# Convolution taps four to a product, with twofold tiles made by DMA, layer norm read from PSUM, and joint first attention scores

## The chip, the cores and the metric

The kernel runs on one core of one Trainium2 chip. The metric is the device time of one execution in microseconds (us). The engines are TensorE (PE, with weight loads shown apart as PEld), VectorE (DVE), ScalarE (ACT), GpSimd (POOL) and SyncE (SP), which only issues DMAs here. Each engine works through its own list of instructions in order and waits for the others by semaphores.

## The reference, cut to what matters

```python
def conformer_conv(h, w_pw1, b_pw1, w_dw, b_dw, ln_g, ln_b, w_pw2, b_pw2):
    u = h @ w_pw1 + b_pw1                     # 512 tokens, 1024 -> 2048
    a, gate = jnp.split(u, 2, axis=-1)
    u = a * jax.nn.sigmoid(gate)
    u = causal_dwconv(u, w_dw, b_dw)          # 31 taps, each feature by itself
    u = jax.nn.silu(layernorm(u, ln_g, ln_b))
    return u @ w_pw2 + b_pw2

for i in range(2):                            # DEPTH = 2
    h = rmsnorm(x, mix_norm_g[i])
    x = x + (conformer_conv(h) if i == 0 else nsa_attention(h))
    x = x + conv_ffn(rmsnorm(x, ffn_norm_g[i]))
```

All is float32 in and out: 512 tokens, 1024 features, 16 heads of 64 in 4 groups. Attention has three branches (compressed, selected, window). With 512 tokens the selected and the window branch each see all earlier tokens, so for each head and each block of 128 queries there are two products of queries with keys, one per branch.

## The kernel before

Activations lie transposed: a tile holds 128 features in its partitions and 512 tokens along its rows, so 1024 features are KT = 8 tiles. A float32 operand of TensorE is split in a high and a low part (ScalarE casts the high part, VectorE subtracts), and `mm3` issues three products: high by high, high by low, low by high.

Four stages follow each other: `conv`, `ffn0`, `attn`, `ffn1`. In `conv`, loop step c projects tile c twice (`project_half`: gate, then value, 24 products each), forms the gated `u` of unit c, and works on the taps of the units before it. The 31 taps of a unit are shared out by the table `CONV`:

- TensorE takes `pe` taps, each as a product with a diagonal matrix, into a `pb` buffer of PSUM (`products`: three products per tap). ScalarE and GpSimd build the diagonals from the identity (`diagonals`, L390 and L393).
- GpSimd takes `pool` taps (`pool_taps`: ScalarE multiplies, L366, GpSimd adds, L368 and L374).
- VectorE takes the rest (`tap`, L345), partly into a `pa` buffer and partly, `late`, on top of TensorE's result.
- `merge` (L405, L406) adds the three sums. It also subtracts the mean of the first unit (`cb`), squares, and GpSimd adds the tiles and squares of units 0 to 6 (L422, L423) for the statistics.

Then comes the layer norm: products with a matrix of 1/1024 and with a column of ones (L490, L493), small vector operations (L502 to L507), a power on GpSimd (L509), a transposition that spreads the result over the partitions, copies of mean and scale from PSUM to SBUF (L499, L511), subtraction, multiplication, Silu, split. The second projection holds all eight outputs in the eight PSUM buffers. `warm` issues products without use in the wait.

PSUM has eight buffers with tags: `pa` 2, `pb` 2, `pf` 3, `po` 1. SBUF slots of 512 columns come from one pool of `NSP` = 55. Within an engine the order of the instructions is set when the kernel is built, by a list scheduler that works with planned durations; the chip keeps this order whatever the durations are. The order of the attention's pieces comes from the table `PLAN`.

In `attn`, `Head.scores` issues for each block of queries the products with the keys of both branches: `G.T` and `G.U` hold two forms of the keys, each branch in its own slot, so that the first two steps have four products each (L1075, L1076). The step's masks and minima follow on VectorE (L1079).

## Time and profile before

| | |
|---|---|
| median of 3 runs | 1302.63 us (1301.27 to 1305.75) |
| the profiled execution | 1305.12 us |
| its span in the trace | 1303.0 us |
| PE busy | 1252.3 us, 96% of the span |
| DVE, ACT, POOL busy | 1034.1, 739.2, 408.2 us |
| `conv` stage | about 0 to 236 us |
| `ffn0`, `attn`, `ffn1` | about 236 to 600, 600 to 937, 937 to 1303 us |

The stages overlap by some us at their borders. Busy time of PE overstates what it does, since matmuls are pipelined: the distance between the starts of two products tells more. A product of 512 columns is shown with 0.39 us, while the next one starts 0.23 us later.

### The profile page before, as it was taken

How to read it: one execution, taken by the hardware profiler on the slowest of the kernel's cores; microseconds unless marked ns; L12 is line 12 of the kernel's file. 1: busy time of each engine (PE TensorE's matmuls, PEld its weight loads, DVE VectorE, ACT ScalarE, POOL GpSimd, SP SyncE). 2: the span in 40 equal slices, each digit the busy share in tenths (PEclk: the TensorE clock that was granted, in tenths of full speed). 3: DMA queues.
4: the chain of work that ended last, by engine and by line, in shares of the span. 5: the costliest groups of instructions: out<-in, count | busy, mean ns of one | idle time of the engine just before them, and what ended most of it. 6: DMA issues, size and time to landing. Idle time of an engine off the chain costs nothing.

```text
span 1303.0 us, 20243 instructions
## 1 busy us (share of the span) xinstructions
PE 1252.3 (96%) x7538; PEld 1105.6 (85%) x7538; DVE 1034.1 (79%) x1777; ACT 739.2 (57%) x1419; POOL 408.2 (31%) x464
## 2 busy tenths in 40 slices
PE   8999789999999999999899999999899999999998
PEld 6887678888999999978888898887688899999996
DVE  6999964689978687775878888888768997778873
ACT  7667733445555455543667778676644465455541
POOL 2668940200200000024557667743220110000000
PEclk9999879999999999999899999999999999999999
DMA  6122102322333232335240101111122232323221
GB/s 232 51 65 65 49 1 81 112 73 81 112 96 112 86 101 97 99 126 156 92 159 35 34 33 34 50 33 41 43 72 79 92 102 92 115 85 126 82 90 73
DMA packets 36946, 109.34 MB, mean 84 GB/s; under 512 B 4208, under 2 KB 4848, under 8 KB 36848
## 3 DMA queue, kind: packets, MB, share of 16 engines
q1 hardware_dynamic: 36848, 108.06, 25.3%
q8 instruction: 59, 0.97, 0.3%
q14 instruction: 39, 0.32, 0.1%
HBM read 103.85 MB, written 2.10 MB: 81 GB/s over the span
## 4 chain that ended last, share of the span: by engine, by line
PE 76%; DVE 11%; POOL 5%; ACT 4%; issue 3%; DMA 1%; SPq 0%; POOLq 0%; ACTq 0%; DVEq 0%
PE pa L631 15%; PE pf L631 7%; PE pb L235 7%; PE pb L236 7%; PE pb L237 6%; PE pf L235 6%; PE pf L236 6%; PE pf L237 6%; PE po L631 4%; POOL s L368 2%; PE pa L237 2%; PE pa L236 2%; PE pa L235 2%; DVE s L231 2%; PE po L1114 2%
## 5 line engine op out<-in xcount | busy, mean ns | idle before, releaser
L646 POOL TENSOR_TENSOR S<-raw 128x512 f32<-128x512 f32 x34 | 53.1, 1562 | 514.3 <-DMA raw<-in_up_dram 297.3
L565 ACT CAST wh<-raw 128x1024 fp32r<-128x1024 f32 (+2 forms) x112 | 95.9, 862 | 84.6 <-PE pb L236 25.5
L566 DVE TENSOR_TENSOR wl<-raw,wh 128x1024 fp32r<-128x1024 f32 (+2 forms) x112 | 114.6, 1030 | 25.8 <-ACT wh L565 25.7
L631 PE MATMUL pa<-s,wh 128*128 128x256 f32 x704 | 129.6, 281 | 0.9 <-ACT wh L565 0.9
L235 PE MATMUL pf<-s,wh 128*128 128x512 f32 x296 | 117.4, 405 | 7.5 <-ACT s L230 3.2
L236 PE MATMUL pf<-s,wh 128*128 128x512 f32 x296 | 118.8, 402 | 0.0
L237 PE MATMUL pf<-s,wl 128*128 128x512 f32 x296 | 118.1, 399 | 0.5 <-DVE wl L225 0.5
L631 PEld LDWEIGHTS pa<-s,wh 128*128 128x128 f32 x704 | 109.9, 189 | 3.5 <-ACT wh L565 1.7
L1090 POOL TENSOR_SCALAR s<-s,cf,gates 128x128 f32<-128x128 f32 (+3 forms) x128 | 79.8, 631 | 79.2 <-DVE cf L1087 66.2
L235 PE MATMUL pb<-s,wh 128*128 128x512 f32 x254 | 99.5, 396 | 2.6 <-ACT s L230 2.4
L236 PE MATMUL pb<-s,wh 128*128 128x512 f32 x254 | 100.3, 395 | 0.0
L237 PE MATMUL pb<-s,wl 128*128 128x512 f32 x254 | 99.8, 394 | 0.0
L631 PE MATMUL pa<-s,wl 128*128 128x256 f32 x352 | 99.1, 281 | 0.0
L224 ACT CAST wh<-raw 128x1024 fp32r<-128x1024 f32 (+1 forms) x60 | 63.2, 1054 | 48.4 <-PE pf L236 28.5
L230 ACT CAST s<-s 128x512 fp32r<-128x512 f32 x84 | 51.7, 619 | 67.2 <-DVE s L580 37.8
L235 PE MATMUL pf<-wh,s 128*128 128x256 f32 (+1 forms) x288 | 83.8, 292 | 4.3 <-DVE v L916 2.6
L1084 ACT ACTIVATE s<-pa,mn 128x128 f32<-128x128 f32 (+3 forms) x128 | 67.4, 531 | 30.1 <-DVE mn L1079 24.0
L236 PE MATMUL pf<-wl,s 128*128 128x256 f32 (+1 forms) x288 | 82.9, 288 | 0.0
L237 PE MATMUL pf<-wh,s 128*128 128x256 f32 (+1 forms) x288 | 82.5, 287 | 0.0
L231 DVE TENSOR_TENSOR s<-s,s 128x512 fp32r<-128x512 f32 x84 | 66.1, 791 | 18.3 <-ACT s L230 18.0
L225 DVE TENSOR_TENSOR wl<-raw,wh 128x1024 fp32r<-128x1024 f32 (+1 forms) x43 | 60.0, 1395 | 22.5 <-ACT wh L224 22.2
L235 PEld LDWEIGHTS pf<-s,wh 128*128 128x128 f32 x296 | 56.4, 191 | 20.8 <-ACT s L230 3.4
(284 smaller groups left out, 3934.1 us busy)
## 6 DMA issues: line engine op xcount, KB each, us to landing
raw<-in_up_dram SPq DMA_DIRECT2D x88, 512.0 KB, 3.6
raw<-in_pw_dram SPq DMA_DIRECT2D x24, 512.0 KB, 3.6
raw<-in_dn_dram SPq DMA_DIRECT2D x48, 256.0 KB, 2.6
raw<-in_dn_dram SPq DMA_DIRECT2D x32, 320.0 KB, 2.8
raw<-in_win_k_dram SPq DMA_DIRECT2D x8, 536.0 KB, 3.5
raw<-in_win_q_dram SPq DMA_DIRECT2D x8, 512.0 KB, 3.5
raw<-in_cw_dram SPq DMA_DIRECT2D x8, 512.0 KB, 3.2
raw<-in_wout_dram SPq DMA_DIRECT2D x8, 512.0 KB, 3.3
```

What stands on the lines that cost most here:

```text
L224: nc.scalar.copy(h[:, :n], raw[:, :n])
L225: (eng or nc.vector).tensor_sub(l[:, :n], raw[:, :n], h[:, :n].bitcast(F32))
L231: nc.vector.tensor_sub(l, src, h.bitcast(F32))
L235: nc.tensor.matmul(out, ah, bh, start=start, stop=False)
L236: nc.tensor.matmul(out, ah, bl, start=False, stop=False)
L237: nc.tensor.matmul(out, al, bh, start=False, stop=stop)
L565: nc.scalar.copy(h, raw)
L566: (eng or nc.vector).tensor_sub(l, raw, h.bitcast(F32))
L631: nc.tensor.matmul(o, p, q, start=start and i + j == 0, stop=i == KT // 2 - 1 and j == 2, skip_group_check=True)
L646: eng[0].tensor_add(s1, a21, a22)
L1084: nc.scalar.activation(a, sv, AF.Exp, scale=-1.0, bias=s.mn[:, c:c + 1], accum_out=s.sums[:, c:c + 1])
L1090: nc.gpsimd.tensor_scalar(a, a, s.cf[:, c:c + 1], gates[:, i, 3 * s.h + 1 + br:3 * s.h + 2 + br], op0=ALU.mult, op1=ALU.mult)
```

## The change

It has four parts.

1. Convolution on TensorE. A product now takes four taps of 64 features. For each unit, `unit` has SP make four twofold tiles (`twice`: two halves of the features, high and low part): the lower 64 partitions hold 64 features, the upper 64 the same features shifted by one token. Each takes two DMAs from SBUF to SBUF and a memset of one column on GpSimd. The weights of such a product have two blocks of output columns, so that it gives two sums, of taps that lie two tokens apart; they land in different partitions, and ScalarE copies them out of two `pa` buffers (L425, L426), one of them to the other half of the partitions, shifted by two tokens. VectorE adds them (`gather`). The weights come from DRAM as `diag` and are split like other weights (L404 to L406), in place of diagonals built on ScalarE and GpSimd. The table changes: TensorE's four-tap groups are 3, 2, 4, 4, 4, 4, 6, 5 per unit (two halves each, three products each), GpSimd's taps 8, 8, 7, 6, 6, 6, 3, 3; VectorE gets the rest.
2. Layer norm from PSUM. Mean and scale are read by VectorE where TensorE left them (`dp`, `rp`), without copies. The last two units go into the statistics by products of their own, instead of an addition on GpSimd. Six outputs of the second projection are held at once, and two follow; a unit is centred into one of two `ctr` buffers, scaled, and split, in turn.
3. Slots. `NSP` falls to 47; `y`, the kept parts of the FFN's combined input (`kept`) and double tiles of the attention (`wide`) have buffers of their own.
4. Attention. The keys of both branches lie side by side in a `wide` tile, and one product covers both branches in the first two steps of a head. The additions in `compress_blocks` take two groups at once.

The core of the diff:

```diff
-CONV = {"pe": [7, 10, 8, 9, 6, 8, 11, 14], "pool": [6, 6, 6, 8, 8, 6, 7, 6], "late": [6, 6, 3, 8, 10, 7, 9, 1], ... "w1": 13, "w2": 9, ...
+CONV = {"pe": [3, 2, 4, 4, 4, 4, 6, 5], "pool": [8, 8, 7, 6, 6, 6, 3, 3], ... "w1": 10, "w2": 6, ...
                 def unit(s, o):
                     c, u = s.c, slot()
                     s.u = u
-                    nc.vector.tensor_mul(u, o, nrm.b)
-                    nc.vector.scalar_tensor_tensor(u, u, v("b_pw1", c), s.y, op0=ALU.add, op1=ALU.mult)
-                    s.uh, s.ul = split(u)
-                    s.sum = ps("pa")
...
+                    nc.vector.tensor_mul(o, o, nrm.b)
+                    nc.vector.scalar_tensor_tensor(u, o, v("b_pw1", c), s.y, op0=ALU.add, op1=ALU.mult)
+
+                    parts = split(u)
+                    s.twice = [[slot(F32R) for _ in parts] for _ in range(2)]
+                    for n, ts in enumerate(s.twice):
+                        for p, t in zip(parts, ts):
+                            rows = p[n * HD:(n + 1) * HD].bitcast(F32)
+                            nc.gpsimd.memset(t[HD:P, 0:1].bitcast(F32), 0.0)
+                            nc.sync.dma_start(t[0:HD, :].bitcast(F32), rows)
+                            nc.sync.dma_start(t[HD:P, 1:S].bitcast(F32), rows[:, 0:S - 1])
...
                 def products(s):
-                    s.pd = ps("pb")
-                    for n, k in enumerate(s.pe):
-                        mm3(s.pd[:, k:S], s.diag[n][0], s.diag[n][1], s.uh[:, 0:S - k], s.ul[:, 0:S - k],
-                            n == 0, n == len(s.pe) - 1)
+
+                    s.pd = [ps("pa") for _ in range(2)]
+                    s.w, s.own = slot(), s.apart and slot()
+                    if not s.apart:
+                        s.sum = ps("pb")
+                    for n in range(2):
+                        for j in range(s.npe):
+                            k = QUAD * j
+                            mm3(s.pd[n][:, k:S], *s.diag[2 * j + n], *(t[:, 0:S - k] for t in s.twice[n]),
+                                j == 0, j == s.npe - 1)
+                        rows = slice(n * HD, (n + 1) * HD)
+                        other = slice((1 - n) * HD, (2 - n) * HD)
+                        if s.apart:
+                            nc.scalar.copy(s.own[rows], s.pd[n][rows])
+                        else:
+                            nc.scalar.activation(s.sum[rows], s.pd[n][rows], AF.Identity, bias=v("b_dw", s.c)[rows])
+                        nc.scalar.copy(s.w[rows, 2:S], s.pd[n][other, 0:S - 2])
+
+                def gather(s):
+                    nc.vector.tensor_add(s.sum[:, 2:S], s.sum[:, 2:S], s.w[:, 2:S])
+                    if s.apart:
+                        nc.vector.tensor_add(s.sum, s.sum, s.own)
...
-                y = units[c].y
-                (nc.vector if c < CONV["sub"] else nc.gpsimd).tensor_sub(y, y, db)
-                nc.vector.tensor_mul(y, y, rb)
...
+            def centre(c):
+
+                cs.append(stage["own"].tile([P, S], F32, tag="ctr", name=nm("ctr"), bufs=NCTR))
+                nc.vector.tensor_sub(cs[c], units[c].y, dp)
+
+            def scale(c):
+                y = cs[c]
+                nc.vector.tensor_mul(y, y, rp)
                 nc.scalar.activation(y, y, AF.Silu, bias=v("ln_b", c), scale=v("ln_g", c))
                 hs.append(split(y))
...
-                        nc.tensor.matmul(sv, q, G.T[br][:, 0:n], start=True, stop=False)
-                        nc.tensor.matmul(sv, q, G.U[br][:, 0:n], start=False, stop=True)
...
+                    for m, t in enumerate((G.T, G.U)):
+                        t = t.rearrange("p (b n) -> p b n", b=2)[:, br:br + nb, 0:n]
+                        nc.tensor.matmul(o[:, 0:nb * n].rearrange("p (b n) -> p b n", b=nb), q, t,
+                                         start=m == 0, stop=m == 1)
```

Where the scheduler puts the work is shown at three places. A name is a tile with its number; two rows with one name touch the same tile.

First TensorE, at the end of the last projection. Before, `pf_1434` is the value half of unit 7, `pb_1398` holds the tap products of unit 6.

```order
L237 MATMUL pf_1434<-s_188,wl_1274 128x512
L235 MATMUL pf_1434<-s_198,wh_1273 128x512
L236 MATMUL pf_1434<-s_199,wh_1273 128x512
L237 MATMUL pf_1434<-s_198,wl_1274 128x512
L236 MATMUL pb_1398<-s_1286,s_1153 128x512
L237 MATMUL pb_1398<-s_1285,s_1154 128x512
```

After, `pf_1357` is the value half of unit 7, `pa_1309` and `pa_1310` hold the sums of unit 6, and `s_1232` and `s_1233` are twofold tiles of unit 6, high and low.

```order
L241 MATMUL pa_1309<-s_1232,dh_1113 128x512
L243 MATMUL pf_1357<-s_188,wl_1222 128x512
L241 MATMUL pf_1357<-s_198,wh_1221 128x512
L242 MATMUL pf_1357<-s_199,wh_1221 128x512
L243 MATMUL pf_1357<-s_198,wl_1222 128x512
L242 MATMUL pa_1309<-s_1233,dh_1113 128x512
```

One product of unit 6 stands ahead of the end of the projection in both, and the rest of unit 6 and all of unit 7 behind it: 74 products before, 65 after.

Second, VectorE behind this point, before: `s_1459` is unit 7's `u`, and `s_1463` its low part.

```order
L355 TENSOR_TENSOR s_1459<-pf_1434,s_270 128x512
L345 SCALAR_TENSOR_TENSOR pa_1289<-s_1282,vec,pa_1289 128x483
L345 SCALAR_TENSOR_TENSOR pb_1216<-s_1108,vec,pb_1216 128x500
L345 SCALAR_TENSOR_TENSOR pb_1216<-s_1108,vec,pb_1216 128x499
L345 SCALAR_TENSOR_TENSOR pb_1216<-s_1108,vec,pb_1216 128x498
L406 TENSOR_TENSOR s_1045<-pb_1216,s_1045 128x512
L225 TENSOR_TENSOR wl_1587<-raw_1584,wh_1586 128x1024
L356 SCALAR_TENSOR_TENSOR s_1459<-s_1459,vec,s_1395 128x512
```

After, `s_1382` is unit 7's `u`, and `s_1386` its low part, from which DMAs make two twofold tiles.

```order
L364 TENSOR_TENSOR pf_1357<-pf_1357,s_254 128x512
L354 SCALAR_TENSOR_TENSOR pb_1160<-s_1059,vec,pb_1160 128x486
L231 TENSOR_TENSOR wl_1502<-raw_1499,wh_1501 128x768
L354 SCALAR_TENSOR_TENSOR pb_1160<-s_1059,vec,pb_1160 128x485
L354 SCALAR_TENSOR_TENSOR pb_1160<-s_1059,vec,pb_1160 128x484
L365 SCALAR_TENSOR_TENSOR s_1382<-pf_1357,vec,y_1306 128x512
L354 SCALAR_TENSOR_TENSOR pb_1160<-s_1059,vec,pb_1160 128x483
L354 SCALAR_TENSOR_TENSOR pb_1160<-s_1059,vec,pb_1160 128x482
L237 TENSOR_TENSOR s_1386<-s_1382,s_1385 128x512
```

In both, work of earlier units and a weight split stand between the two operations that form unit 7's `u`: six instructions before, four after.

Third, TensorE at the first scores of the first head, before.

```order
L1075 MATMUL pa_6785<-s_6641,s_6545 128x128
L1075 MATMUL pa_6823<-s_6641,s_6545 128x256
L1076 MATMUL pa_6785<-s_6647,s_6545 128x128
L1075 MATMUL pa_6785<-s_6642,s_6545 128x128
L1076 MATMUL pa_6823<-s_6647,s_6545 128x256
L1075 MATMUL pa_6823<-s_6642,s_6545 128x256
L1076 MATMUL pa_6785<-s_6650,s_6545 128x128
L1076 MATMUL pa_6823<-s_6650,s_6545 128x256
```

After:

```order
L1133 MATMUL pa_6697<-wide_6531,s_6459 128x256
L1133 MATMUL pa_6733<-wide_6531,s_6459 128x512
L1133 MATMUL pa_6697<-wide_6532,s_6459 128x256
L1133 MATMUL pa_6733<-wide_6532,s_6459 128x512
```

Four products of twice the columns stand where there were eight.

## Rows read from the trace of the kernel before

**Rows 1.** The page, busy time of each engine.

```profile
PE 1252.3 (96%) x7538; PEld 1105.6 (85%) x7538; DVE 1034.1 (79%) x1777; ACT 739.2 (57%) x1419; POOL 408.2 (31%) x464
```

**Rows 2.** Windows of `conv`: busy us by engine, PEclk, DMA share, GB/s.

```profile
100.00:120.00 20.00, 20.00 (x89) 16.47 (x88) 20.00 (x27) 15.58 (x38) 18.72 (x19) 1.00 0.14 41
...
140.00:160.00 20.00, 12.73 (x48) 9.58 (x47) 19.86 (x26) 17.09 (x36) 19.76 (x25) 0.85 0.16 54
...
155.00:160.00 5.00, 3.56 (x8) 2.51 (x9) 5.00 (x7) 4.79 (x8) 5.00 (x6) 0.50 0.05 20
```

**Rows 3.** Timeline of PE, 141 to 193: start, us, line, tiles, [idle before].

```profile
141.33 0.40 PE L237 MATMUL pf<-s,wl 128*128 128x512 f32 x1
141.84 0.50 PE L236 MATMUL pb<-s,s 128*128 128x512 f32 x1
...
148.90 0.38 PE L237 MATMUL pb<-s,s 128*128 128x482 f32 x1
155.00 0.76 PE L235 MATMUL pb<-s,s 128*128 128x512 f32 x1 [5.72 <-issue]
...
167.97 0.38 PE L237 MATMUL pb<-s,s 128*128 128x482 f32 x1
171.31 2.07 PE L490 MATMUL pa<-s,avg 128*128 128x512 f32 x2 [2.96 <-POOL s L422]
...
190.14 0.50 PE L235 MATMUL po<-s,wh 128*128 128x512 f32 x1 [0.51 <-ACT s L230]
...
192.90 0.50 PE L236 MATMUL po<-s,wh 128*128 128x512 f32 x1 [0.66 <-DVE s L231]
```

**Rows 4.** The chain that ended last, in order of time: start, us, what.

```profile
141.23 5.71 POOL s L390 x13
```

**Rows 5.** Groups of DVE by form, 40 to 195: count, busy us, mean ns.

```profile
L225 DVE TENSOR_TENSOR wl<-raw,wh 128x1024 fp32r<-128x1024 f32 x13 | 19.7, 1518 | 0.0
...
L356 DVE SCALAR_TENSOR_TENSOR s<-s,vec,s 128x512 f32<-128x512 f32 x7 | 8.9, 1274 | 0.0
...
L345 DVE SCALAR_TENSOR_TENSOR pa<-s,vec,pa 128x483 f32<-128x483 f32 x8 | 5.7, 712 | 0.0
...
L523 DVE TENSOR_TENSOR s<-s,s 128x512 f32<-128x512 f32 x8 | 4.9, 685 | 2.9 <-ACT s L511 2.9
L355 DVE TENSOR_TENSOR s<-pf,s 128x512 f32<-128x512 f32 x7 | 4.8, 679 | 1.7 <-PE pf L237 1.7
...
L507 DVE TENSOR_SCALAR var<-var 128x4 f32<-128x4 f32 x1 | 0.2, 169 | 0.0
```

**Rows 6.** Two DMA lines of `attn`, SBUF to SBUF, 64 partitions: ns min/median/max on SP.

```profile
L793 SPq DMA_DIRECT2D s<-s x8: 527/571/602, 605.6 to 614.7; - x8
...
DMA to landing us min/median/max: 2.2/2.4/3.2
...
L794 SPq DMA_DIRECT2D s<-s x8: 584/600/1272, 606.2 to 615.3; - x8
```

**Rows 7.** Groups of ACT by form, 40 to 195.

```profile
L524 ACT ACTIVATE s<-s,vec 128x512 f32<-128x512 f32 x8 | 6.1, 807 | 0.8 <-DVE s L523 0.8
...
L499 ACT COPY s<-pa 128x512 f32<-128x512 f32 x1 | 0.6, 586 | 3.1 <-PE pa L490 3.1
```

**Rows 8.** Groups of POOL by form, 40 to 195.

```profile
L509 POOL TENSOR_TENSOR rs<-var,mhalf 128x4 f32<-128x4 f32 x1 | 1.0, 1029 | 1.9 <-DVE var L507 1.9
```

**Rows 9.** Timeline of PE in `attn`, two first steps of scores and what follows.

```profile
748.60 0.27 PE L1075 MATMUL pa<-s,s 128*128 128x128 f32 x1
...
749.05 0.62 PE L1098 MATMUL pb<-ident,s 128*128 128x128 f32 x4
...
755.92 0.28 PE L1075 MATMUL pa<-s,s 128*128 128x256 f32 x1
...
756.40 0.60 PE L956 MATMUL pf<-ident,t 128*128 128x128 f32 x4
```

**Rows 10.** Windows, the heads of `attn`.

```profile
680.00:940.00 260.00, 245.12 (x1596) 216.84 (x1595) 216.22 (x605) 193.37 (x491) 152.49 (x232) 0.99 0.11 38
```

More of the change, by code (lines that the diff above doesn't have):

```diff
@@ L333, in __init__ @@
                     s.c = c
-                    s.pe = [0] + PE_SHIFTS[len(PE_SHIFTS) + 1 - CONV["pe"][c]:]
-                    rest = [k for k in range(2, TAPS) if k not in s.pe]
+                    s.npe = CONV["pe"][c]
+                    rest = list(range(QUAD * s.npe, TAPS))
                     n = CONV["pool"][c]
-                    s.pool, dve = rest[:n], rest[n:]
-                    n = CONV["late"][c]
-                    s.early, s.late = dve[n:], dve[:n]
+                    s.apart = c == KT - 1
+                    if s.apart:
+                        s.one = rest.pop(0)
+                    s.pool, s.dve = rest[:n], rest[n:]
                 def wt(s, shift):
@@ L484, in conv_module, with second @@
                     Z.merge()
-            wp2 = [load_split(A["pw2"][k]) for k in range(4)]
+            def second(k):
+                return load_split(A["pw2"][k], MF * P)
+            wp2 = [second(k) for k in range(4)]
             last = units[KT - 1]
             st, dp = ps("pb"), ps("pa")
-            for n, (a, q) in enumerate(((stat["y"], stat["q"]), (last.y, last.q))):
-                nc.tensor.matmul(dp, avg, a, start=n == 0, stop=n == 1)
+            groups = [(stat["y"], stat["q"])] + [(units[c].y, units[c].q) for c in range(KT - APART, KT)]
+            for n, (a, q) in enumerate(groups):
                 for j, t in enumerate((a, q)):
@@ L509, in conv_module @@
             nc.gpsimd.tensor_tensor(rs, var, mhalf[:, 0:NB], op=ALU.pow)
+            tiny = small(1, "tiny", 1)
+            nc.scalar.activation(tiny, last.q[:, 0:1], AF.Silu)
+            warm(CONV["w1"], "pf", last.q)
             rp = spread(rs, "po")
-            nc.scalar.copy(rb, rp)
-            warm(CONV["w2"], "pf", rb)
-            outs = [ps(t) for t in [t for t in ("po", "pb", "pf", "pa") for _ in range(NPS[t])]]
-            hs = []
-            def out_half(m, k, w):
-                sl = slice(m * P, (m + 1) * P)
-                mm3(outs[m], w[0][:, sl], w[1][:, sl], hs[k][0], hs[k][1], k == 0, k == KT - 1)
@@ new lines, in conv_module @@
+            outs = [ps(t) for t in ("pf", "pf", "pf", "pb", "pa", "pb")]
+            centre(0)
+            for k in range(KT):
+                if k + 1 < KT:
+                    centre(k + 1)
+                scale(k)
+                w = wp2[k]
+                for m in range(MF):
+                    sl = slice(m * P, (m + 1) * P)
+                    mm3(outs[m], w[0][:, sl], w[1][:, sl], *hs[k], k == 0, k == KT - 1)
+                if k < 4:
+                    wp2.append(second(4 + k))
+                elif k < 6:
+                    wp2.append(load_split(A["pw2b"][k - 4]))
```

174 lines of the change are left out of this document (94 added, 80 removed).

## The prediction

> **What bounds the kernel now.** I read the page first: PE is busy 1252 of 1303 us, DVE as the next one 1034 [rows 1]. So the question is where PE issues fewer products, and where it now stands still. I then cut `conv` into windows of 20 us and followed PE by its timeline. From about 33 to 141 us PE is full: 89 products in 20 us, one every 0.225 us, at a granted clock of 1.00; DVE is full in the same window too [rows 2]. [...] Then PE waits 2.96 us for GpSimd's last sum and runs the statistics, and the second projection starts at 190.14 and is steady from 192.90 [rows 3]. Eight products lie between these two; at 0.23 each they would end a steady start at 192.90 - 8 x 0.23 = 191.06. So 141.33 to 191.06 is 49.7 us in which PE has work for 74 products, 16.4 us. In the heads of the attention PE is busy 245 of 260 us [rows 10].
>
> **The change part by part.** Everything below uses 0.22 us for a product of 512 columns or a little less.
>
> *Tap products beside the projections.* Of units 0 to 5 PE took 7+10+8+9+6+8 = 48 taps, 144 products; now it takes 3+2+4+4+4+4 = 21 groups, each two halves, three products: 126. That is 18 x 0.22 = **-4.0 us**, if PE stays full. SP now issues 8 copies per unit, at 0.57 to 0.60 us, 4.7 us [rows 6]; a unit lasts some 14 us, and the weight loads need only some issues besides, so I cost them at nothing. ScalarE gets two half copies more, 0.6 each by [rows 7], and loses diagonals; GpSimd loses diagonals and gets two small sets of a column per half; both had and keep time. What would end the cover is a unit's `u` coming late.
>
> Does DVE keep up? From the first `u` to unit 7's projection its list has 116 instructions. At some 0.64 to 0.71 us for an operation of 512 columns and 1.1 to 1.5 for a weight split [rows 5] they come to about 81 us. PE has 450 products in that stretch, 450 x 0.225 = 101 us. So DVE has 20 us of slack on the whole, where before it had none. But the order is fixed: adding up both lists row by row, I find one place where PE gets ahead. The gate projection of unit 6 needs a `pf` buffer that unit 4's second operation (L365) has to free, and this one stands behind a group of taps. I take **+1.8 us** for it; 0 and 6 are the bounds (6 if three more units have such a place). For units 1 to 6 the last of a unit's twofold tiles lands, by the same sum and a landing of 2.4 us [rows 6], 3.3 to 5 us before PE comes to it.
>
> *From the last projection to the last tap.* Before: 167.97 - 141.33 = 26.6 us. After, counted from the end of the projection: L364 0.68, a tap 0.71, a split of 768 columns about 1.1 (between 0.68 and 1.52), two taps 1.4, L365 0.68 [rows 5]: `u` at 4.6. The first order of VectorE above shows this. ScalarE casts the high part by about 5.6, behind a copy of unit 6's first sum. L365 has now an operand in PSUM, so I take 0.68, not the 1.27 of the operation it replaces, which had two in SBUF [rows 5]; if it is 1.27 all this is 0.6 later. The first pair of copies: 0.57 + 0.60 of issue and 2.4 to land: 9.2. Each further pair is 1.2 later, 10.4, 11.5 and 12.7. PE meanwhile has 35 products of unit 6, 35 x 0.22 = 7.7, then waits until 9.2 for the first product of unit 7 and until 10.4 for the second, which takes the low part; the second half's tiles come before PE needs them (10.4 + 14 x 0.22 = 13.5). The 29 further products end at 10.4 + 29 x 0.22 = 16.8. PE's clock fell to 0.50 in the stretch that holds a wait of 5.72 us; two waits of 1.0 to 1.5 us follow here. I take 8 of these products at half clock, +1.8: 18.6. **-8.0 us.** Bounds: no half clock -9.8; copies at 3.2 and all 29 products at half clock, 11.2 + 29 x 0.44 = 24, so -2.6.
>
> *From the last tap to the second projection.* Before: 191.06 - 167.97 = 23.1 us. What goes: the wait of 2.96 for GpSimd, the two copies to SBUF (0.59 for the one shown) [rows 7], and the scaling of units in a row. What remains as a chain: two half copies 1.2, three additions on VectorE 2.0, a square 0.7, products for the last unit's statistics 0.8 (two products of another kind took 2.07 [rows 3], the upper bound), four small operations at 0.17 [rows 5] 0.7, the power 1.03 [rows 8], spreading over the partitions 0.6 (between 0.17 and 2.07), centring and scaling 1.4, Silu 0.81 and the cast 0.59 [rows 7], 1.4: sum 9.8. Ten hand-overs between engines cost something each; 0.5 to 0.66 us is what PE waits in such steps of the start [rows 3], but most of this is work that I already count. I take 0.2 each: 12. **-11 us**, between -14 (9 us) and -7 (16 us, all hand-overs at the full 0.6).
>
> [...]
>
> *Attention.* One head had four products of 128 columns within 748.60 to 749.05, 0.45 us, and four of 256 within 755.92 to 756.40, 0.48 us [rows 9]. Two products of 256 take half of the latter, 0.24: -0.21. Two of 512 take 2 x 0.23 = 0.46: -0.02. 16 heads x 0.23 = 3.7 us. PE is busy 94% there [rows 10], so most of this counts: **-3.0 us**. The pieces' order changes too, so +3 and -5 are the bounds. The rest of the program has the same products (the second projection's 192 as well), and the slots are dealt out otherwise but not fewer than are used; I cost this at nothing.
>
> Sum: -4.0 + 1.8 - 8.0 - 11.0 - 3.0 = -24.2 us. The profiled execution took 1305.12, so 1280.9; it lies 2.5 us above the median of the runs, so **1278 us** against 1302.6.
>
> **The rivals.** About 0.3% (4 us) is what a measurement of this kernel can tell from no change.
>
> *A smaller gain, 10 to 15 us, near 1290.* The same mechanisms, but the copies' way into unit 7 (7 steps from PSUM over VectorE, ScalarE, SP and DMA to PE) eats the tail: at the bounds above the tail gives 2.6 + 7 instead of 19, and with stalls of 4 in the middle 4.0 - 4 + 9.6 + 2 = 11.6 us remain. For it: the chain before already shows how a late `u` and a half clock come together. Against: 8 copies issued in 9 us landed in at most 3.2 us [rows 6].
>
> *Copies queue behind weight loads.* SP issues the weights of the second projection in the same list. The DMA engines move 54 GB/s at a share of 0.16 there [rows 2], so at full share a load of 0.5 MB takes about 0.16 x 20 x 0.5/1.08 = 1.5 us; a copy behind one or two such loads is 1.5 to 3 us late, unit 7 too: 1280 to 1281. This is inside the forecast's range. [...]
>
> *A larger gain, near 1270.* No stall in the middle (1.8), no half clock (1.8), chain at its short end (3), and the attention at -5 (2): 24.2 + 8.6 = 33 us.
>
> *Slower.* One mechanism: PE's list has the first twofold product of a unit in the middle of another projection, so a late copy stops the projection as well. If copies beside the weight traffic of `conv` land in 10 us instead of 2.4, units 1 to 6 each wait 7.6 - 3.3 = 4.3 us and lose some 1.8 by the clock (as taken for unit 7), and unit 7 comes 7.6 later with as much again: 6 x 6.1 + 9.4 = 46 us against 24 gained (+22, 1324). It decides from a landing of about 7.1 us: six waits of 1.4 with 1.8 of clock, and 4.7 at unit 7, take the 24. For it: no copy of this form runs beside these loads before. Against: the DMA share there is 0.14 to 0.16.
>
> *It does nothing.* The saved time at the tail could come back if the second projection waits for weights or for the splits of the eight units; before, its first products wait 0.5 to 0.66 us for those only [rows 3].
>
> **How the numbers follow.** Forecast (1272 to 1285) 0.57; smaller gain 0.20; larger gain 0.15; nothing 0.03; slower 0.05. The time is the forecast's. The range, 1267 to 1292, takes in the larger and most of the smaller gain: about 0.86 by these, and the bounds of the unknown terms lie within it. Faster: 0.57 + 0.20 + 0.15 = 0.92.
>
> **What the profile of the changed kernel would show.** Right: PE at one product per 0.225 us to the end of the last projection, at about 139 us; a wait of 1 to 3 us, not 5.7, before unit 7's products, ended by a DMA; the last tap some 18.6 us behind the projection and the second projection steady some 12 us later, at about 170; the heads of the attention 3 us shorter; the feed-forward stages as long as before. Wrong: PE waiting for twofold tiles in the middle of projections; copies that land later than 3.2 us; a granted clock of 0.50 over most of unit 7; more than 16 us between last tap and second projection; an attention that isn't shorter.

## The result and the profile after

The changed kernel takes 1289.33 us (median of 4 runs, 1287.37 to 1292.05) against 1304.14 us in runs taken beside it: a ratio of 0.989, 95% interval 0.9863 to 0.9918. It is faster by some 15 us (11 to 18), inside the forecast's range (1267 to 1292) but near its upper end; the forecast time was 1278. A second set of five runs of the same kernel gave 0.9889 (0.9874 to 0.9904). The profiled execution took 1289.72 us, its span is 1287.9.

The page, busy time by engine, answers to [rows 1]:

```profile
PE 1242.8 (96%) x7447; PEld 1092.9 (85%) x7447; DVE 1012.0 (79%) x1727; ACT 728.5 (57%) x1337; POOL 375.5 (29%) x435
```

The timeline of PE behind the last projection (start, us, tiles, idle before), which answers to [rows 3]. `pf` is the last projection, `pa<-s,dh` are tap products, L527 and L529 the statistics, L213 products without use, L306 the spreading of the scale; the last row is the second projection's start:

```profile
135.29 0.39 PE L243 MATMUL pf<-s,wl 128*128 128x512 f32 x1
...
143.24 0.38 PE L243 MATMUL pa<-s,dl 128*128 128x492 f32 x1
146.55 0.47 PE L241 MATMUL pa<-s,dh 128*128 128x512 f32 x1 [2.93 <-ACT dh L405]
147.77 0.77 PE L242 MATMUL pa<-s,dh 128*128 128x512 f32 x1 [0.75 <-DMA s<-s]
...
155.73 0.39 PE L243 MATMUL pa<-s,dl 128*128 128x496 f32 x1
...
161.30 1.69 PE L527 MATMUL pb<-ones,y 128*128 128x1 f32 x8
162.85 1.85 PE L527 MATMUL pb<-ones,s 128*128 128x1 f32 x8
...
166.40 3.23 PE L213 MATMUL pf<-s,ident 128*128 128x128 f32 x20
169.46 0.60 PE L306 MATMUL po<-ident,rs 128*128 128x128 f32 x4
...
172.90 0.96 PE L241 MATMUL pf<-s,wh 128*128 128x512 f32 x3 [1.45 <-ACT s L236]
```

The wait of 2.93 us before unit 7 is put down to a cast on ScalarE, but it is the copies that end it: the copy issued at 144.06 lands at 146.41 and the product starts 0.14 us later, the one issued at 145.34 lands at 147.64 and the second product starts 0.13 us later.

Put beside the forecast, stage by stage (us between the same two places in both profiles):

| from, to | before | after | difference | forecast |
|---|---|---|---|---|
| start, first steady product of the projections | 33.05 | 31.80 | -1.25 | 0 |
| to the last projection product | 108.3 | 103.5 | -4.8 | -2.2 |
| to the last tap product | 26.6 | 20.4 | -6.2 | -8.0 |
| to the second projection | 23.1 | 17.2 | -5.9 | -11.0 |
| to the compression in `attn` | 469.6 | 468.7 | -0.9 | 0 |
| to the output projection | 274.9 | 275.0 | +0.1 | -3.0 |
| to the end | 367.4 | 371.3 | +3.9 | 0 |

The sum is -15.05, the difference of the spans. Of the convolution's forecast gain of 21.2 us, 18.2 are there (1.25 of them ahead of the place where it was forecast); the attention gives nothing, and 3.9 us are lost in a part that the change does not touch.

The output projection starts at these places, before and after:

```profile
935.57 1.56 PE L235 MATMUL pf<-s,wh 128*128 128x512 f32 x3 [3.21 <-ACT s L230]
```

```profile
916.57 1.65 PE L241 MATMUL pf<-s,wh 128*128 128x512 f32 x3 [3.20 <-ACT s L236]
```

The same stretch on the other engines of the changed kernel: unit 7's way into its twofold tiles, and the layer norm:

```profile
138.03 0.69 DVE L364 TENSOR_TENSOR pf<-pf,s 128x512 f32<-128x512 f32 x1
...
142.02 0.75 DVE L365 SCALAR_TENSOR_TENSOR s<-pf,vec,y 128x512 f32<-128x512 f32 x1
...
142.86 0.62 ACT L236 CAST s<-s 128x512 fp32r<-128x512 f32 x1 [2.00 <-DVE s L365]
...
158.90 0.69 DVE L436 TENSOR_TENSOR y<-pb,y 128x512 f32<-128x512 f32 x1
...
165.57 1.03 POOL L538 TENSOR_TENSOR rs<-var,mhalf 128x4 f32<-128x4 f32 x1 [12.70 <-DVE var L536]
```

VectorE comes to the last projection at 138.03, 2.3 us behind its last product's end; `u` is ready 7.5 us behind that product's start. The sum of unit 7 is ready at 159.59, but TensorE's products on it end at 164.7, and the power ends at 166.60 while the spreading starts at 169.46.

All 32 first copies (lower half) of the twofold tiles, issue time on SP in ns, and landing:

```profile
L373 SPq DMA_DIRECT2D s<-s x32: 461/546/680, 34.4 to 147.3; - x32
...
DMA to landing us min/median/max: 2.2/2.3/3.6
```

VectorE by form in the full stretch, 60 to 140 us (count, busy, mean ns):

```profile
L231 DVE TENSOR_TENSOR wl<-raw,wh 128x1024 fp32r<-128x1024 f32 x6 | 9.4, 1568 | 0.0
L406 DVE TENSOR_TENSOR dl<-dr,dh 128x1024 fp32r<-128x1024 f32 x4 | 7.5, 1863 | 0.0
L231 DVE TENSOR_TENSOR wl<-raw,wh 128x768 fp32r<-128x768 f32 x4 | 5.9, 1478 | 0.0
L237 DVE TENSOR_TENSOR s<-s,s 128x512 fp32r<-128x512 f32 x5 | 5.8, 1160 | 0.0
```

And two windows of the changed kernel, from the first steady product to the end of the last projection, and in the statistics (columns as in [rows 2]):

```profile
31.80:135.70 103.90, 103.83 (x442) 84.11 (x443) 91.36 (x113) 71.49 (x109) 71.17 (x82) 0.98 0.54 148
...
162.00:164.00 2.00, 2.00 (x11) 2.00 (x11) 0.00 (x0) 0.00 (x0) 0.00 (x0) 0.50 0.00 0
```

### The profile page after: what moved, and what is told of

Its sections match the earlier page's. It is cut to its first block, busy times and chain, and to the rows that moved or that the text cites. A ratio compares the mean times of both kernels' runs of the same rounds, so it can differ in the third digit from the quotient of the medians.

```text
span 1287.9 us, 20149 instructions
## 1 busy us (share of the span) xinstructions
PE 1242.8 (96%) x7447; PEld 1092.9 (85%) x7447; DVE 1012.0 (79%) x1727; ACT 728.5 (57%) x1337; POOL 375.5 (29%) x435
## 4 chain that ended last, share of the span: by engine, by line
PE 83%; DVE 7%; ACT 5%; POOL 2%; issue 2%; DMA 1%; SPq 0%; ACTq 0%; DVEq 0%; POOLq 0%
PE pa L685 15%; PE pf L685 8%; PE pf L241 7%; PE pf L242 7%; PE pf L243 6%; PE pb L241 6%; PE pb L242 6%; PE pb L243 6%; PE po L685 4%; PE pa L242 3%; PE pa L241 3%; PE pa L243 2%; PE po L1173 2%; PE pa L1133 2%; PE pb L1157 2%
## 5 line engine op out<-in xcount | busy, mean ns | idle before, releaser
L700 POOL TENSOR_TENSOR S<-raw 128x512 f32<-128x512 f32 x34 | 54.5, 1604 | 516.9 <-DMA raw<-in_up_dram 275.2
L616 ACT CAST wh<-raw 128x1024 fp32r<-128x1024 f32 (+2 forms) x112 | 95.9, 862 | 86.5 <-PE pb L242 26.4
L617 DVE TENSOR_TENSOR wl<-raw,wh 128x1024 fp32r<-128x1024 f32 (+2 forms) x112 | 113.8, 1023 | 27.7 <-ACT wh L616 27.4
L230 ACT CAST wh<-raw 128x1024 fp32r<-128x1024 f32 (+2 forms) x62 | 63.5, 1025 | 40.4 <-PE pf L242 21.9
L236 ACT CAST s<-s 128x512 fp32r<-128x512 f32 x76 | 47.0, 619 | 60.0 <-DVE s L631 37.6
L231 DVE TENSOR_TENSOR wl<-raw,wh 128x1024 fp32r<-128x1024 f32 (+2 forms) x45 | 60.7, 1350 | 18.9 <-ACT wh L230 18.7
L237 DVE TENSOR_TENSOR s<-s,s 128x512 fp32r<-128x512 f32 x76 | 62.0, 816 | 14.6 <-ACT s L236 14.4
L750 DVE TENSOR_TENSOR x<-pb,x 128x512 f32<-128x512 f32 x80 | 53.9, 684 | 24.4 <-PE pb L243 24.2
L1138 DVE CUSTOM_DVE_ANT_0 pa<-pa,tab 128x128 f32<-128x128 f32 (+3 forms) x128 | 62.6, 494 | 11.8 <-PE pa L1133 10.7
L617 DVE TENSOR_TENSOR l<-raw,h 128x1024 fp32r<-128x1024 f32 (+2 forms) x56 | 58.5, 1045 | 15.6 <-ACT h L616 15.4
```

The source lines that it names most:

```text
L230: nc.scalar.copy(h[:, :n], raw[:, :n])
L231: (eng or nc.vector).tensor_sub(l[:, :n], raw[:, :n], h[:, :n].bitcast(F32))
L237: nc.vector.tensor_sub(l, src, h.bitcast(F32))
L616: nc.scalar.copy(h, raw)
L617: (eng or nc.vector).tensor_sub(l, raw, h.bitcast(F32))
L1138: nc.vector.tensor_tensor_reduce(sv, sv, mask[:, S - n:S], 1.0, 3e38, op0=ALU.add, op1=ALU.min, accum_out=s.mn[:, c:c + 1])
```

## The experiments

Twelve further runs (e9 is the changed kernel once more), in three groups: e1 to e4, e5 to e8 and e9 to e12, each on one chip. Each ratio is taken against runs of the kernel before on the same chip (medians 1303.74, 1304.34 and 1303.82). Within one group the time of one kernel differs by 1.6 to 8 us from execution to execution, and from kernel to kernel the stretch with a granted clock of 0.50 in the statistics begins elsewhere (at 161.3 in the changed kernel, 160.0 in e10, 158.8 in e6); so for effects of 1 to 3 us I read stage times in the profiles as well.

| run | median us | ratio, 95% interval | last tap to spreading |
|---|---|---|---|
| changed kernel | 1289.33 | 0.989 (0.9863 to 0.9918) | 13.73 |
| e1 scores apart | 1285.36 | 0.9863 (0.9832 to 0.9893) | 16.99 |
| e2 fewer idle products | 1287.47 | 0.9875 (0.9853 to 0.9897) | 13.35 |
| e3 unit 7's copies twice | 1290.23 | 0.9902 (0.9876 to 0.9929) | 11.77 |
| e4 less on VectorE | 1292.05 | 0.9901 (0.9874 to 0.9927) | 16.69 |
| e5 no idle products | 1286.14 | 0.9861 (0.984 to 0.9882) | 10.67 |
| e6 idle products in the wait | 1292.04 | 0.9898 (0.9875 to 0.9922) | 20.56 |
| e7 layer norm with copies | 1287.69 | 0.9869 (0.9849 to 0.9889) | 13.79 |
| e8 unit 6 added by GpSimd | 1286.94 | 0.9864 (0.9829 to 0.9899) | 17.89 |
| e9 changed kernel again | 1288.78 | 0.9889 (0.9874 to 0.9904) | 13.68 |
| e10 idle products behind | 1282.83 | 0.9843 (0.9826 to 0.986) | 11.21 |
| e11 the same, scores apart | 1283.35 | 0.9845 (0.9828 to 0.9863) | 11.00 |
| e12 more taps on TensorE | 1297.24 | 0.9953 (0.9937 to 0.9969) | 13.55 |

### The joint scores: e1 and e11

```diff
-                    for m, t in enumerate((G.T, G.U)):
-                        t = t.rearrange("p (b n) -> p b n", b=2)[:, br:br + nb, 0:n]
-                        nc.tensor.matmul(o[:, 0:nb * n].rearrange("p (b n) -> p b n", b=nb), q, t,
-                                         start=m == 0, stop=m == 1)
+                    for b in range(nb):
+                        for m, t in enumerate((G.T, G.U)):
+                            t = t[:, (br + b) * S:(br + b) * S + n]
+                            nc.tensor.matmul(o[:, b * n:(b + 1) * n], q, t, start=m == 0, stop=m == 1)
```

e1:

> The changed kernel with four products in each of the first two steps of a head, as before, and all else as it is. My prediction gave the joint scores 3.0 us: 16 heads x 0.23 less 6%; then this kernel takes 3 us more than the changed one, 1292. The rival, from the two traces: the time from the first scores to the last values fell by only 2.0 us (from 681.6 to 932.1 before, from 664.6 to 913.1 after), so the heads are held by the work of ScalarE, VectorE and GpSimd for a part of the time, and this kernel takes 1 to 2 us more, 1290 to 1291. If it takes as long as the changed one, the 2.0 us came from the other order of the pieces.

e11 has this edit on top of e10's (below):

> The kernel with the 12 small products behind the spreading, and the first scores of each branch apart as before the change. If the joint scores are worth nothing, as the run with them apart alone showed, it takes as long as the one with them joint (within 1.5 us), and the stretch from the first scores to the last values takes 244.5 to 246.5 us in both. If my prediction's 3.0 us are there after all and were covered by chance in that run, it takes 2 to 3 us more.

Both medians with the scores apart are no higher than those with them joint (1285.36 against 1289.33, 1283.35 against 1282.83). The heads from first scores to last values, in windows of e10 (joint) and of e11 (apart):

```profile
664.10:910.80 246.70, 233.91 (x1494) 204.76 (x1492) 204.03 (x592) 187.32 (x479) 150.21 (x229) 0.99 0.11 35
```

```profile
662.10:908.30 246.20, 236.94 (x1561) 210.54 (x1559) 204.76 (x594) 187.57 (x482) 149.59 (x229) 0.99 0.11 35
```

TensorE is busy 236.94 - 233.91 = 3.03 us less with joint scores, the 3.0 us that I forecast. But the stretch is no shorter: the saving has become waiting (246.7 - 233.9 = 12.8 us against 246.2 - 236.9 = 9.3). The longest waits of PE in the heads of the changed kernel (us in total, times, longest):

```profile
PE pb L1157 <- DVE s L237: 3.7, 5, 1.6
PE pa L1133 <- ACT s L1143: 3.2, 5, 1.5
```

Before, the same two lines had 2.4 and 0.8 us. So PE's longest waits in the heads are now for the splits on VectorE and the exponentials on ScalarE, whose number the joint scores leave as it was; that these set the length is read from the waits, no run made them shorter. From compression to output projection the eleven profiles with joint scores behind the change take 272.9 to 275.2 us, the two with scores apart 275.1 and 275.0. The means are 274.2 and 275.1: the forecast 3 us are not there, and a gain of about 1 us can't be told from this spread.

### Idle products ahead of the spreading: e2, e5, e10

e2 changes `"w1": 10` to `"w1": 2`, e5 sets both counts to 0.

> The changed kernel with 2 instead of 10 products without use between the statistics and the spreading of the scale. In the trace they take 166.40 to 169.46, while the power on GpSimd ended at 166.60; before the change the spreading began 0.5 us behind the power. Theory: they stand in the way, the spreading begins at about 167.2, and the second projection 2.3 us earlier: 1287. Rival: these products are what brings the granted clock from 0.50 back to 1.00 at 168; without them the spreading and the first products of the second projection run at 0.50, and the time is the same or up to 2 us more.

In e2 the spreading came only 0.35 us earlier. Its timeline shows why:

```profile
166.51 1.06 PE L213 MATMUL pf<-s,ident 128*128 128x128 f32 x4
...
167.22 2.05 PE L211 MATMUL pf<-idle 128*128 128x512 f32 x6
...
169.11 0.60 PE L306 MATMUL po<-ident,rs 128*128 128x128 f32 x4
```

The scheduler put the other six products without use in the free place, so the run did not tell the theories apart.

> The changed kernel without products without use between the statistics and the second projection (both groups, 10 and 6, are gone; with 2 and 6 the six came ahead of the spreading in place of the ten, so that run didn't clear the way). Theory: TensorE's list held the spreading up from 167.1 to 169.46; now it begins 0.5 us behind the power on GpSimd, as before the change, and from last tap to second projection it takes 14.8 instead of 17.2 us at the same granted clock. Rival: without them the granted clock stays at 0.50 into the second projection, and this takes back 1.5 us or more.

GpSimd's power, the spreading and the second projection in e5's timeline:

```profile
165.37 1.03 POOL L538 TENSOR_TENSOR rs<-var,mhalf 128x4 f32<-128x4 f32 x1 [12.50 <-DVE var L536]
...
166.45 1.12 PE L306 MATMUL po<-ident,rs 128*128 128x128 f32 x4
...
170.44 1.65 PE L241 MATMUL pf<-s,wh 128*128 128x512 f32 x3 [2.87 <-ACT s L236]
```

Here the way is clear: the spreading starts 0.05 us behind the power's end, and from last tap to second projection it takes 14.66 instead of 17.17 us. The rival's half clock is there too. The window of e5 at the start of the second projection:

```profile
170.00:175.00 5.00, 4.56 (x11) 3.59 (x12) 3.69 (x6) 2.31 (x4) 0.00 (x0) 0.50 0.00 0
```

11 products in 5 us at 0.50, and from second projection to the feed-forward stage it takes 111.7 instead of 109.5 us. What the clear way gave, 2.5 us, the half clock took back but for 0.25.

e10 takes both groups out and repeats the spreading three times without use, behind itself:

```diff
-"w1": 10, "w2": 6
+"w1": 0, "w2": 0
             rp = spread(rs, "po")
+            for _ in range(3):
+                spread(rs, "pf")
```

> The changed kernel with the 16 products without use taken out ahead of the spreading of the scale, and 12 small ones of 128 columns put behind it, where TensorE waited 2.9 us for the first unit in the kernel without any. Theory: the 3 us that the spreading gained there stay (last tap to spreading 10.7 instead of 13.7), and the granted clock is back at 1.00 when the second projection begins, so that the 2.3 us which that kernel lost again in its second projection stay as well: 1285 to 1286.5, and the way from last tap to the feed-forward stage 2 us shorter than the 126.4 of both. Rival: small products do not bring the clock back: 126.4 again.

PE in e10, the small products and the first of the second projection:

```profile
166.62 1.58 PE L306 MATMUL pf<-ident,rs 128*128 128x128 f32 x12
169.70 0.98 PE L241 MATMUL pf<-s,wh 128*128 128x512 f32 x3 [1.50 <-ACT s L236]
```

And the window of e10 behind it:

```profile
170.00:175.00 5.00, 5.00 (x23) 4.05 (x22) 3.36 (x6) 2.31 (x4) 0.00 (x0) 1.00 0.01 3
```

The second projection runs at 1.00 from its start, and from last tap to feed-forward stage it takes 124.7 us (124.4 in e11) instead of 126.6 (126.5 in e9). Whether the small products brought the clock back isn't shown. It rose between these two windows of e10, 0.2 us after the first of them began:

```profile
163.40:166.80 3.40, 3.35 (x9) 1.78 (x10) 1.76 (x6) 0.00 (x0) 1.03 (x1) 0.50 0.00 0
166.85:169.70 2.85, 1.34 (x13) 1.10 (x11) 1.36 (x4) 2.08 (x4) 0.00 (x0) 1.00 0.00 0
```

In the kernel without any, e5, the clock had fallen 1.5 us later (161.5 instead of 160.0) and stayed at 0.50 until 175.2.

1282.83 us is the best time of all, below the 1285 to 1286.5 that I expected, and its interval does not touch that of e9, the changed kernel on the same chip. Of the 6 us between the two medians some 2 lie in this stretch. Even these are not seen to last: from last tap to the compression in `attn` e10 takes 486.6 us and e11 484.3, the changed kernel 485.9 and 485.8 in its two profiles. The rest is in other stages (below).

### The copies into unit 7: e3

Each pair of unit 7's copies is issued a second time, directly behind itself.

```diff
                             nc.sync.dma_start(t[HD:P, 1:S].bitcast(F32), rows[:, 0:S - 1])
+                            if c == KT - 1:
+                                nc.sync.dma_start(t[0:HD, :].bitcast(F32), rows)
+                                nc.sync.dma_start(t[HD:P, 1:S].bitcast(F32), rows[:, 0:S - 1])
```

> The changed kernel with unit 7's eight copies issued twice, each pair directly behind itself. Theory: the way of the copies (issue on SyncE, then landing) sets when TensorE goes on with unit 7. The high part comes no later (or 1.2 us, if the second writing is waited for), the low part 2.3 us later, and with it all of unit 7, so 2 to 3.5 us more: 1291 to 1293. Rival: VectorE's lateness or the statistics set the end, the copies don't: the same time as the changed kernel.

Unit 7's first two products in e3's timeline, and the issue of the copy on SP that the second one needs (L377 is the added line):

```profile
148.50 0.76 PE L241 MATMUL pa<-s,dh 128*128 128x512 f32 x1 [5.12 <-DMA s<-s]
149.07 0.46 SPq L377 DMA_DIRECT2D s<-s  x1
...
151.41 0.76 PE L242 MATMUL pa<-s,dh 128*128 128x512 f32 x1 [2.15 <-POOL y L391]
```

The last tap is 4.7 us later behind the last projection (25.1 against 20.4): the copies are on the path. It is more than the 2 to 3.5 of issue alone, since SP wrote the tile again only when the first copy had landed (the first lands at 145.53, its second writing is issued at 145.54). (The second wait is put down to GpSimd; but the copy issued at 149.07 lands at 151.28, and PE goes on 0.13 us later.) But the median is only 1 us above the changed kernel's. In the profile 2.0 of the 4.7 us come back by the second projection, where the statistics ran at full clock this time, and 3.4 behind the output projection, where the changed kernel is slow (below, e9). The window 160 to 165 of e3, and then two of e1:

```profile
160.00:165.00 5.00, 5.00 (x38) 4.46 (x37) 2.09 (x3) 2.09 (x4) 0.00 (x0) 1.00 0.00 0
```

```profile
160.00:165.00 5.00, 5.00 (x19) 3.97 (x19) 0.00 (x0) 1.46 (x2) 0.00 (x0) 0.50 0.00 0
165.00:170.00 5.00, 5.00 (x18) 3.97 (x19) 1.95 (x6) 0.00 (x0) 1.03 (x1) 0.50 0.00 0
```

From last tap to spreading the changed kernel and e1 have the same instructions in the same order on all engines: 13.7 us with a part at half clock (0.50 in 162 to 164), 17.0 with most of it at half. So the clock alone moves this stretch by 3.3 us. e3, at full clock, takes 11.8, but in another order: its statistics are interleaved otherwise, and the six products without use stand ahead of the spreading.

### VectorE's lateness: e4

```diff
-                    s.pool, s.dve = rest[:n], rest[n:]
+                    s.pool, s.dve = rest[:n], rest[n + (2 if 2 <= c < 6 else 0):]
```

> The changed kernel without the first two of VectorE's taps in each of units 2 to 5 (8 taps left out, so the sum of the convolution lacks them): some 5.8 us less of work on VectorE ahead of unit 7. Theory: VectorE, full from 60 to 140 us, comes 2.7 us late to unit 7's last projection, so unit 7's u comes 2 to 3 us earlier here, and the last tap too: 1286 to 1287. Rival: VectorE's lateness costs nothing, since TensorE has unit 6's products meanwhile and the copies and the clock set the rest: within 1 us of the changed kernel.

This is inconclusive. `u` is ready 7.3 us behind the last projection's last product, instead of 7.5, since the scheduler used the free place on VectorE for weight splits and later taps; the last tap lies 20.7 us behind it, and the median is no lower. What an early VectorE would bring is not shown by it; that a later copy delays the last tap is, by e3.

### Idle products in the wait: e6

A `warm(6, "pf")` after each group of statistics but the last, which the scheduler moves forward into the wait for unit 7's copies.

> The changed kernel with 12 products of 512 columns without use, which stand in TensorE's list (one beside the last projection's end, eleven behind unit 6's taps) where TensorE waits for unit 7's copies. Theory: the wait is 4.3 us in the changed kernel, so 11 x 0.22 = 2.4 us fit into it and cost nothing, and the granted clock stays at 1.00 for unit 7's first products, of which 8 ran at 0.50 (0.42 instead of 0.22 us): the last tap 1.0 to 1.6 us earlier behind the last projection, 18.9 to 19.4 instead of 20.4. Rival: the clock of these products doesn't hang on the wait: the last tap at 20.4 or later.

The idle products and unit 7's first one in e6's timeline, and then two windows of e6:

```profile
144.03 2.67 PE L211 MATMUL pf<-idle 128*128 128x512 f32 x11
...
147.68 0.47 PE L241 MATMUL pa<-s,dh 128*128 128x512 f32 x1 [0.98 <-DMA s<-s]
```

```profile
149.00:156.00 7.00, 7.00 (x30) 5.66 (x31) 7.00 (x11) 2.61 (x5) 4.04 (x4) 1.00 0.25 57
...
165.00:170.00 5.00, 5.00 (x19) 3.97 (x19) 0.00 (x0) 0.00 (x0) 0.00 (x0) 0.50 0.00 0
```

Unit 7 now runs at 1.00 throughout, and the last tap comes 19.7 us behind the last projection although unit 7's first product came 0.8 us later behind it: 0.7 us gained where 1.0 to 1.6 were expected. It did not help the time: the statistics ran at 0.50 from 158.8 on, and VectorE's order changed as well (unit 6's sum came later), 20.6 us from last tap to spreading.

### The layer norm: e7 and e8

e7 copies mean and scale to SBUF again (`nc.scalar.copy(db, dp)`, `nc.scalar.copy(rp, spread(rs, "po"))`).

> The changed kernel with the mean and the scale copied from PSUM to SBUF by ScalarE, as before the change. My prediction counted both copies as gone from the chain, 1.2 us. From the trace: the mean's copy lies beside the power on GpSimd (1.03 us) and the idle products, so only the scale's copy counts, 0.6 us from spreading to second projection (3.4 becomes 4.0). Rival: if reading PSUM by VectorE is slower, the subtractions and multiplications get faster with the copies, and the 0.6 shrinks.

Spreading to second projection takes 4.07 instead of 3.44 us: 0.63, one copy. The first two subtractions of the mean, from SBUF in e7 and from PSUM in the changed kernel:

```profile
167.41 1.29 DVE L553 TENSOR_TENSOR ctr<-y,s 128x512 f32<-128x512 f32 x2 [1.77 <-ACT s L541]
```

```profile
166.65 1.28 DVE L550 TENSOR_TENSOR ctr<-y,pa 128x512 f32<-128x512 f32 x2 [1.15 <-PE pa L529]
```

So the rival falls.

e8 sets `APART = 1`.

> The changed kernel with only the last unit in the statistics by products of its own; unit 6 is added by GpSimd (two additions of 1.26 us), as all units but one were before. Theory: in the changed kernel TensorE gets to unit 7's statistics 1.7 us after its sum is ready (159.6, 161.3), since unit 6's own products stand ahead; GpSimd's additions end at about the same time as unit 7's sum. So this kernel is as fast from last tap to spreading at the same clock, within 1 us. Rival (the products of unit 6 bring what the prediction credits to them): the wait for GpSimd comes back, 2 to 3 us.

PE's first statistics in e8:

```profile
157.79 1.67 PE L527 MATMUL pb<-ones,s 128*128 128x1 f32 x8 [1.93 <-POOL s L454]
```

The wait for GpSimd is back (1.9 us), and last tap to spreading takes 4.2 us more than in the changed kernel. By the comparison with e1 most of that is the clock, which fell 2.6 us behind the last tap in e8 and was at 0.50 for the rest of its statistics (1.71 to 1.84 us for a group of eight). In e1 it fell 3.3 us behind the last tap and stayed low as long (some 13.6 us); e1, with `APART = 2`, takes 17.0 us, so e8 is only 0.9 us longer. This is inside the 1 us that I had expected at the same clock. The wait is the rival's, its 2 to 3 us are not shown.

### The kernel again, and more taps: e9, e12

> The changed kernel itself once more, for a second profile. Three things of the first profile should tell chance from order. Of the order, so here again: the wait of 1.64 us at the beginning of the second feed-forward stage (its instructions stand in another order there than in all the variants so far), the wait before unit 7's products, the last tap some 20.4 us behind the last projection. Of chance, so not here again in the same places: the stretches at a granted clock of 0.50 (the start of the projections, the statistics, the output projection), which cost the first profile some 1 to 3 us at each place. Median as before, 1289 within 2.

All three of the order came again: the wait before unit 7 (2.9 and 0.8 us), 20.5 us to the last tap, and in the feed-forward stage

```profile
992.31 0.50 PE L241 MATMUL pb<-s,wh 128*128 128x512 f32 x1 [1.65 <-ACT s L236]
```

No other run has this wait, nor had the kernel before. From output projection to the end the changed kernel takes 371.3 and 370.7 us, the eleven others 367.8 to 369.5, the kernel before 367.4. In all eleven the order of TensorE's products there differs from the changed kernel's, which is the same in its two profiles. So some 2 to 3 us of the lost 3.9 go with the order that the scheduler happened to give this kernel there; the clock is another: in the output projection the products follow each other at 0.43 us, as at 0.50, until 922.1 in the first profile and until 920.5 in this one. The half clock at the start and in the statistics came in about the same places again, so there it was not chance alone.

e12 sets `pe` of units 2 and 3 to 5.

> The changed kernel with one group of four taps more on TensorE in units 2 and 3 (12 products more; 8 taps less on VectorE, some 5.8 us). Theory: TensorE sets the time between the projections, so the last projection ends 12 x 0.225 = 2.7 us later, 106.2 instead of 103.5 us behind the first steady product. Rival: VectorE, full there too, sets it: no later, or earlier. In this kernel VectorE's list has the addition of unit 6's second sum ahead of the first operation on unit 7's last projection; it waits for unit 6's products on TensorE, so unit 7's u comes 11 to 13 us behind the last projection instead of 7.5, and the last tap 24 to 26 instead of 20.4. Together 5 to 8 us more than the changed kernel, 1294 to 1297.

The last product of the last projection, and unit 7's first, in e12:

```profile
145.16 0.40 PE L243 MATMUL pf<-s,wl 128*128 128x512 f32 x1
152.65 0.76 PE L241 MATMUL pa<-s,dh 128*128 128x512 f32 x1 [7.09 <-DMA s<-s]
```

8.5 us more than e9. The scheduler put unit 6's products ahead of the projection's end as well, so this mark moved by 35 products more, and my times behind it (`u`, last tap) don't apply. Counted by products, 488 from the first steady one took 112.3 us, 0.230 each; in e5 and e10, whose first steps ran at full clock, 441 took 102.05, 0.231 each. VectorE had 8 taps less (74.1 us busy from 60 to 140, 79.0 in the changed kernel) and PE's pace did not change: TensorE sets the time between the projections. With nothing left for PE to do meanwhile, the wait for unit 7's tiles is 7.1 us instead of 3.7.

## Why the prediction held, and where its terms were off

The sign was right, and so were the mechanisms in the convolution: fewer tap products, and a shorter wait for unit 7 that ends with a copy (2.93 and 0.75 us, where [rows 3] has 5.72 and [rows 4] shows GpSimd at 13 diagonals). The forecast gain was 24.2 us and 15.05 came. Too little came from the layer norm (5.1 us), the last stage (3.9), the attention (3.1) and the way to the last tap (1.8), 13.9 us together; 4.8 us came in other places where I had forecast less or nothing. So the range held in part by luck, since errors in both directions met in the sum. Of the five signs of being wrong that I had named three were there: more than 16 us from last tap to second projection (17.2), an attention that isn't shorter, and copies that land later than 3.2 us (up to 3.6). The last was a poor sign: of the copies before, the eight that [rows 6] shows without a landing had landed in up to 3.5 us.

**Tap products beside the projections.** 441 products stand where 459 stood, as forecast, and PE had no wait there: the stall of +1.8 did not come, its lower bound of 0 was the truth. e12 confirms the price of a product (0.230 us). The start, 1.25 us earlier, is chance: over the runs the first steady product lies between 31.4 and 33.3.

**VectorE's slack was smaller than I summed up, and in the wrong place.** Forecast 81 us for its list, measured 91.4 busy of 103.9 (the window above). Of the 12.5 us left, 11.5 lie ahead of 60 us, and from 60 to 140 it was full (79.0 of 80 us). The splits were mis-sized: 768 columns take 1.48 us where I took 1.1, a split of the tap weights 1.86. A split of 512 columns took 1.16 us here, and 0.65 at 172.88 (two in 1.29), where GpSimd did nothing. No run here took GpSimd's work away, so its part in this is not shown, and these rows stay unexplained. VectorE came to the last projection 2.7 us after its last product's start; the six operations from there to `u` took 4.7 us, as forecast (4.6). So `u` of unit 7 came at 7.5 instead of 4.6 us. The choice for L365 was right: 0.74 us with an operand in PSUM, not the 1.27 of [rows 5].

**The last tap**, 20.4 instead of 18.6 behind the projection: the 2.9 us of `u`, less 0.8 since cast and first copies were quicker than forecast (3.8 us from `u` to first product instead of 4.6), and 0.3 less in unit 7's products. The half clock was as forecast, 8 products at 0.42; at 1.00 the products of unit 7 followed each other at 0.227 us in e6, where the forecast has 0.22. Landing at 2.2 to 3.6 us, 2.3 in the median, settles the rivals on slow copies: the DMA share from the first steady product to the end of the last projection rose from 0.18 to 0.54, and the copies landed as quickly as in [rows 6]. Of a wait behind a weight load, on which one of these rivals rests, at most 3.6 - 2.3 = 1.3 us is in these rows; that a copy waited for such a load at all no run shows.

**From last tap to second projection**, 17.2 instead of 12. This is the step that failed most. (a) The statistics: from unit 7's sum to TensorE's last column of them I had 0.7 + 0.8 us; measured 5.1 (159.59 to 164.70). Unit 6's products stood ahead (1.7 us), and one group of eight took 1.7 to 1.85 us at 0.50, 0.9 at 1.00 (the group at 158.57, followed at 159.46). I had seen the half clock in [rows 2] and priced it only for the tap products. The price stood in the trace of the kernel before, where a granted clock of 0.50 held for these products too, in a row that the prediction does not use:

```profile
173.18 1.71 PE L493 MATMUL pb<-ones,s 128*128 128x1 f32 x8
```

A unit needs two such groups, so my 0.8 for both was less than half of their price at full clock (1.8) and a quarter of that at 0.50 (3.4). (b) The products without use: 2.9 us between power and spreading, where I had one hand-over of 0.2. I took `warm` for work that fills a wait; in TensorE's fixed order it was work ahead of the path, as e5 shows (0.05 us between power and spreading without it). Together with 0.7 in the sum of unit 7 these are some 7 us; the other hand-overs that I had added on top, some 2 us, are contained in the measured pieces, and 5.2 remain. The sum of unit 7 (3.9 us against 3.2) was nearly right, and reading from PSUM cost nothing in these rows (1.28 us for the first two subtractions of the mean, 1.29 from SBUF in e7), but only one of the two copies saves time (e7).

**Attention.** The term was the busy time of TensorE, and exactly that was saved (3.03 us); the step that failed is "PE is busy 94% there, so most of this counts". The longest of PE's waits there end with VectorE and ScalarE, and the saved time went into waiting (12.8 against 9.3 us in e10 and e11). The stretch from compression to output projection is unchanged (274.9, 275.0 us), and e1 and e11 show no gain of the joint scores that can be told from the spread of the profiles.

**The last stage** was costed at nothing and lost 3.9 us, by another order of the same instructions and the clock, as far as the profiles of e9 and the others tell. It hides a fifth of the gain: the convolution alone, from start to second projection, is 18.2 us shorter.

So the outcome is the rival of the smaller gain, by other causes than the one I gave it: not slow copies, but the layer norm's chain and an attention that TensorE doesn't bound.

## What to carry to other kernels

A product without use that stands ahead of the work on the path in an engine's list can itself be part of the path (here 2.9 us between power and spreading, 0.05 in e5), and it pays to look in the built order where the scheduler put it. A saving on an engine that is 94% busy can be worth nothing where the longest waits in the other 6% are for engines that the edit leaves as they are (here 3.03 us saved, and heads of 246.7 against 246.2 us): price it in the stretch's length. Before pricing a chain, look for its own instructions in the trace of the kernel before, at the clock that they had there (here 1.71 us for eight products at 0.50). And when a scheduler rebuilds the whole order, look for what the edit did to stages that it doesn't touch, by a second profile of the same kernel.

## What the runs showed that I had not expected

The granted clock makes one chain of instructions in one order 13.7 or 17.0 us long (the changed kernel twice, and e1), a spread of 3.3 us. It is one reason why medians within 3 us of each other had to be told apart by stage times. In the one profile where a wait was filled the half clock came in the next stretch instead, and for longer (e6: 0.50 from 158.8 to 175.9). And with twelve small products behind the spreading the second projection began at 1.00 in two kernels (e10, e11), without any at 0.50 in one (e5); what makes the difference stays open.
